# Second block: where the decay's exponentials stand on ScalarE, the pace of the chain of heads, and where the condition's rows live

## The chip, the cores and the metric

The kernel runs on one NeuronCore of one Trainium2 chip. The metric is the device time of one launch in microseconds (us), lower is better; the time before is the median of three runs. Engines are named as the profile names them: PE is TensorE (PEld its weight loads), DVE is VectorE, ACT is ScalarE, POOL is GpSimd, SP is SyncE, which here issues DMAs.

## The reference, cut to what matters

One sequence of 256 positions and 1024 channels goes through a first block of two layers and then a second block of two layers. The change is in the second block, but for one buffer of the first (`mod` below: the condition's rows). All matrix products are float32.

```
def first_block(x, c, ...):
    c_act = silu(c)
    for l in range(2):
        mod = c_act @ w_ada[l] + b_ada[l]      # the condition
        ...

def second_block(x, ...):
    for l in range(2):
        z = rms_norm(x) @ w_in[l]
        (cq, ckv, kpe, gq, gk, gv, glr, gr, su, gates) = split(z)
        o_a = mla_mixer(cq, ckv, kpe)          # 8 heads, causal softmax
        o_b = gla_mixer(gq, gk, gv, glr, gr)   # below
        o_c = s5_mixer(su)                     # diagonal state space, gelu, then a gated product w_glu
        g = sigmoid(gates + gate_b)            # 3 x 1024 wide
        x = x + (g0 * (o_a @ w_br_mla) + g1 * (o_b @ w_br_gla) + g2 * (o_c @ w_br_s5)) @ w_out[l]
        x = x + square(relu(rms_norm(x) @ w_ff1[l])) @ w_ff2[l]

def gla_mixer(q, k, v, g_lr, r):
    log_a = log_sigmoid(g_lr @ w_gate + b_gate) / 16
    bc = cumsum(log_a, within chunks of 64)
    q_t, k_t, k_end = q * exp(bc), k * exp(-bc), k * exp(bc_last - bc)
    ... # chunked products with v, a state carried over four chunks
```

## The kernel before

**Weights and products.** Weights stream from HBM in tiles of 128x1024 (`raw`, 5 buffers, loaded by SP). Each is split into two parts whose sum is the float32 value: `whi` by a copy on ACT (L463, 4 buffers) and `wlo = raw - whi` on DVE (L464, 3 buffers). `lin_t` computes one output tile of 128x256 from eight weight slices with 24 matmuls, three for each slice (L499, L500, L501); a product over four slices has 12. The results stand in one of four PSUM buffers (`pmm`); short products and transposes use four others (`px`). A fifth user of `pmm` has to wait until the first has been read.

**The second block's order.** `block2(l)` is written as a program, and a scheduler sets each engine's queue from it by readiness and priority; each engine then works its own queue in order. The projection `w_in_2` gives in turn the latents, the s5 input `u` and `gr`, then the sources of the attention's q, k and v (L1579 to L1585). Then, at L1596 to L1604, the decay: `log1pexp_neg` on DVE (L676 to L683), L1599, L1600 and eight cumulative sums (L1604, `TENSOR_TENSOR_SCAN`) into `bc`, followed by ten exponentials on ACT: `eb` (L1606), `en` (L1609) and eight pieces of `ke` (L1611). Their two 128x512 tiles are named `ge` in the profile. Then the values `gv` (`lin_n`, two `pmm` buffers) with two copies on ACT (L1617).

After that a loop over 24 gates: each is one `lin_t` (24 matmuls) and one tanh on ACT (L1693) that frees its `pmm`. Ahead of gate 4 stands `linear_qk` (four tiles, scaled by `eb`, `en` and `ke` on DVE). Ahead of each gate `paced(chain, CHAIN)` writes the next steps of a generator, `chains()`: eight steps of `mla_heads` (for each half of the heads, for q and k, for two row tiles: L1650, the rotary lines L805 to L811 and L1655 on DVE give `mq3`, which four transposes L689 turn two steps later and a copy L690 on ACT reads), then `gla` (L1772 to L1837: products `am`, the states `gst` as a chain of ACT and DVE steps, then the output), then the attention (L827 to L862). `paced` ties a step to the last matmul and the last `wlo` written so far.

At every third gate one step of `s5_run` is written. It has four rounds q = 0 to 3. A round is: four products L1464 with the tile `ur`; copies and products on ACT and DVE (L1466 to L1470); eight scans (L1475); copies and products again (L1477 to L1481) that end in `vb`; four matmuls L1489 and eight L1493; a copy `yj` (L1496); a DMA to HBM (L1497) and two back (L1500, issued by SP); and the update of `uT[:, q]` (L1504). What is left of the rounds after the gates is written after the branch products of gla and mla (eight tiles of 12 matmuls each). Then come gelu (L1717) and the split `yhlh` (L554) of each `uT[:, q]`, and the gated product `s5_w_glu_2` that contracts over the four q, q = 3 last (four tiles of 12 matmuls).

**Buffers.** `slot()` gives 128x1024 float32 tiles from a pool of `NSLOT` = 20. `crow`, the condition's rows of the first block, has a 128x1024 tile of its own for the whole program.

Of the kernel before, what the change touches and what calls it, by code (L numbers as in the profile page):

```python
# [19 lines left out]
F32 = mybir.dt.float32  # L20
F32R = mybir.dt.float32r
I32 = mybir.dt.int32
AF = mybir.ActivationFunctionType
# [325 lines left out]
def program(ctx: ExitStack, tc: tile.TileContext, a, out, pp_at, cst_at):  # L349
    nc = tc.nc  # L350
    V, S, G, PE, SY = nc.vector, nc.scalar, nc.gpsimd, nc.tensor, nc.sync

    cpool = ctx.enter_context(tc.tile_pool(name="cpool", bufs=1))
# [4 lines left out]
    ps_x = ctx.enter_context(tc.tile_pool(name="psx", bufs=1, space=bass.MemoryType.PSUM))  # L358
    dram = ctx.enter_context(tc.tile_pool(name="dram", bufs=1, space=bass.MemoryType.DRAM))

    NSLOT = 20
    NFILL = 4
    PUP = 6
    PDN = 2
# [4 lines left out]
    NTH = 2  # L369
    NSC = 2  # L370
    LAG = 2
    CHAIN = 2
    REST_AT = 6
    PRIO = 1500

# [13 lines left out]
    cact = cpool.tile([128, 8], F32, name="cact")  # L389
    xns = [slots.tile([128, 4, 256], F32, name="xn", tag="s4", bufs=NSLOT) for _ in range(2)]  # L390
    xns = [x.rearrange("p a b -> p (a b)") for x in xns]
# [16 lines left out]
    def P(key, j=None):  # L408
        o, n = pp_at[key]
        p, o = (pp[0], o) if o < PP0 else (pp[1], o - PP0)  # L410
        return p[:, o:o + n] if j is None else p[:, o + j:o + j + 1]
# [4 lines left out]
    def slot(dt=F32, name="s4"):  # L416
        return slots.tile([128, 4, 256], dt, name=name, tag="s4", bufs=NSLOT)

# [3 lines left out]
    def t256(name="t256", dt=F32):  # L422
        return tmp.tile([128, 256], dt, name=name, tag="t256", bufs=N256)
# [66 lines left out]
    def lin_t(name, src, kts, m=128, parts=(128,), n=T, ps=None):  # L490

        ps = pmm() if ps is None else ps
        kts = list(kts)
        for q, kt in enumerate(kts):
            if parts == (128,):
                wh, wl = weight(m, name)
            else:
                wh, wl = joined([(weight(c, name), st["last"])[1] for c in parts])
            PE.matmul(ps[:m, :n], wh, src.hi(kt), start=q == 0, stop=False)  # L499
            PE.matmul(ps[:m, :n], wh, src.lo(kt), start=False, stop=False)  # L500
            st["mm"] = PE.matmul(ps[:m, :n], wl, src.hi(kt), start=False, stop=q == len(kts) - 1).ins  # L501
        return ps

    def paced(gen, n=1):

        for _ in range(n):
            with tc.issue_after(st["mm"]), tc.issue_after(st["lo"]):
                next(gen, None)
# [17 lines left out]
    def lin_n(name, src, kts, n):  # L526

        ps = [pmm(), pmm()]
        kts = list(kts)
        for q, kt in enumerate(kts):  # L530
            add_n(ps, src, kt, weight(n, name), q == 0, q == len(kts) - 1)
        return ps
# [221 lines left out]
        V.tensor_reduce(norms[0].ss, sqs, AX.X, OP.add)  # L754


    crow = cpool.tile([128, 1024], F32, name="crow")
    for q in range(2):
        pc = px()
        for j in range(4):  # L760
# [745 lines left out]
    def block2(l):  # L1506
        w = "w_in_2"
        flat = lambda x: x.rearrange("p a b -> p (a b)")
# [86 lines left out]
        for j in range(2):  # L1595
            S.activation(la[:, j * 256:(j + 1) * 256], pa[:, j * 256:(j + 1) * 256], AF.Identity,  # L1596
                         bias=P(("bg", l), j))
# [4 lines left out]
        bc, eb = ges[:, 0:512], ges[:, 512:1024]  # L1602
        for q in range(8):
            V.tensor_tensor_scan(bc[:, q * 64:(q + 1) * 64], ones[:, :64], la[:, q * 64:(q + 1) * 64], 0.0,  # L1604
                                 OP.mult, OP.add)
        S.activation(eb, bc, AF.Exp)  # L1606
        ges2 = flat(slot(name="ge2"))
        en, ke = ges2[:, 0:512], ges2[:, 512:1024]
        S.activation(en, bc, AF.Exp, scale=-1.0)  # L1609
        for q in range(8):  # L1610
            S.activation(ke[:, q * 64:(q + 1) * 64], bc[:, q * 64:(q + 1) * 64], AF.Exp,  # L1611
                         bias=bc[:, q * 64 + 63:q * 64 + 64], scale=-1.0)
        next(steps)
        gv = flat(slot(name="gv"))
        gvN = [gv[:, t * 512:(t + 1) * 512] for t in range(2)]
        for t, p_ in enumerate(lin_n(w, h, range(8), 512)):
            S.activation(gvN[t], p_, AF.Copy)  # L1617
        gqk = slot(name="gqk")
        gqf, gkf = flat(gqk[:, 0:2, :]), flat(gqk[:, 2:4, :])

        def linear_qk():
            for j in range(2):
                js = slice(j * 256, (j + 1) * 256)
                ps = lin_t(w, h, range(8))
                V.scalar_tensor_tensor(gqf[:, js], ps[:, :T], 0.125, eb[:, js], OP.mult, OP.mult)
            for j in range(2):
                js = slice(j * 256, (j + 1) * 256)
                ps = lin_t(w, h, range(8))
                V.tensor_tensor(gkf[:, js], ps[:, :T], en[:, js], OP.mult)
                V.tensor_tensor(ke[:, js], ps[:, :T], ke[:, js], OP.mult)  # L1630
# [33 lines left out]
        def chains():  # L1664
            for hf in range(2):
                yield from mla_heads(hf)
            while late:
                yield
                f_, *args = late.pop(0)
                f_(*args)  # L1670
            ob.append(new_hl(4, "ob"))
            yield from gla(l, eb, gqf, gkf, ke, gvN, gr, ob[0])
            oa.append(new_hl(4, "oa"))
            yield from attention((0, 4), lambda hh: heads[hh // 4]["q"][:96, hh % 4, :],
                                 lambda hh: heads[hh // 4]["k"][:96, hh % 4, :], 96 ** -0.5,
                                 lambda t: C("caus")[:, 128 - 128 * t:],
                                 lambda t, hh: vs[:, hh // 4, t, hh % 4], oa[0])
# [4 lines left out]
        gates, chain = {}, chains()  # L1682
        for n in range(24):
            if n == GQK_AT:
                linear_qk()
            paced(chain, CHAIN)
            if n % 3 == 2:
                paced(steps)
            br, j = (1, 0, 2)[n // 8], n % 8
            if j % 4 == 0:  # L1690
                gates.setdefault(br, []).append(slot(name="gate"))
            ps = lin_t(w, h, range(8))
            S.activation(gates[br][j // 4][:, j % 4, :], ps[:, :T], AF.Tanh,  # L1693
                         bias=gbh[:, br * 8 + j:br * 8 + j + 1], scale=0.5)
# [27 lines left out]
        for j in range(4):  # L1722
            ps = lin_t("s5_w_glu_2", yhl, range(4))
            t = t256("oc")
# [117 lines left out]
    for l in range(2):  # L1842
        block2(l)
# [28 lines left out]
```

## Time and profile before

| | |
|---|---|
| median of three runs | 2246.64 us (2245.1 to 2252.94) |
| the profiled execution | 2245.79 us, span 2243.8 us |
| mean granted clock of PE | 0.98 of full speed |
| PE busy | 2140.3 us, 95% of the span |
| PEld busy | 2024.6 us, 90% |
| DVE busy | 1732.6 us, 77% |
| ACT busy | 1336.3 us, 60% |
| POOL busy | 116.5 us, 5% |

PE sets the time: what counts is where PE stands idle or runs at half clock, and that is read from the timeline of PE, from what ended its waits, and from short windows with their granted clock. The second block's layer 0 has its decay and gates at 1380 to 1530 us of the span, layer 1 at 1840 to 2010 us. A timeline row gives start, length, engine, line, operation, tiles, count, and in brackets the idle time just before and what ended it.

### The profile page before, as it was taken

The page shows a single profiled execution, that of the slowest core. Times are in us where ns is not written, and L with a number is a line of the kernel's source. Part 1 is how long each engine was busy: PE and PEld are TensorE (multiplying, and loading weights), DVE is VectorE, ACT ScalarE, POOL GpSimd, SP SyncE. Part 2 cuts the span into 40 slices and gives each one's busy share as a digit, 9 for nine tenths or more (in the row PEclk, how much of TensorE's full clock was granted, in tenths as well). Part 3 has the DMA queues.
Part 4 walks back from the last instruction along what each step waited for, and adds up shares of the span by engine and source line. Part 5 has one row for each costly group of instructions (what it writes and reads, how often), then busy time and mean ns, then how long its engine had stood idle before and what let it go on. Part 6 is the DMA issues. An engine that isn't in the chain of part 4 may idle for free. (4 is left out here: it accounts for less than half of the span.)

```text
span 2243.8 us, 44306 instructions
## 1 busy us (share of the span) xinstructions
PE 2140.3 (95%) x17296; PEld 2024.6 (90%) x17296; DVE 1732.6 (77%) x3349; ACT 1336.3 (60%) x2461; POOL 116.5 (5%) x122
## 2 busy tenths in 40 slices
PE   7998999999998997999989999899999997999999
PEld 6888789998997886889989998899999997999999
DVE  4888888889887888788889787677875577678753
ACT  4546866466646557775576566585664464755643
POOL 0210011000000210011000001000000010000000
PEclk9999999999999998999999999899999998999999
DMA  8755344856685653444746666444555564444553
GB/s 324 246 206 197 138 166 152 296 198 208 224 286 188 225 190 132 167 162 164 263 159 199 200 242 225 135 157 158 177 190 182 174 218 135 150 160 162 195 180 123
DMA packets 143457, 429.09 MB, mean 191 GB/s; under 512 B 34864, under 2 KB 40976, under 8 KB 143248
## 3 DMA queue, kind: packets, MB, share of 16 engines
q1 hardware_dynamic: 136496, 422.24, 55.4%
q10 hardware_dynamic: 6752, 4.02, 0.6%
q8 instruction: 136, 2.23, 0.4%
q14 instruction: 73, 0.60, 0.1%
HBM read 413.98 MB, written 12.22 MB: 190 GB/s over the span
## 5 line engine op out<-in xcount | busy, mean ns | idle before, releaser
L463 ACT ACTIVATE whi<-raw 128x1024 fp32r<-128x1024 f32 x639 | 674.8, 1059 | 592.4 <-PE pmm L500 356.1
L464 DVE TENSOR_TENSOR wlo<-raw,whi 128x1024 fp32r<-128x1024 f32 x639 | 781.8, 1225 | 295.0 <-PE pmm L501 161.8
L499 PE MATMUL pmm<-hh,whi 128*128 128x256 f32 x2432 | 698.3, 288 | 31.8 <-ACT fh L554 14.9
L501 PE MATMUL pmm<-hh,wlo 128*128 128x256 f32 x2432 | 693.0, 286 | 4.1 <-DVE wlo L464 4.1
L500 PE MATMUL pmm<-hl,whi 128*128 128x256 f32 x2432 | 694.2, 286 | 0.0
L499 PEld LDWEIGHTS pmm<-hh,whi 128*128 128x128 f32 x2432 | 470.0, 194 | 40.8 <-ACT fh L554 15.2
L501 PEld LDWEIGHTS pmm<-hh,wlo 128*128 128x128 f32 x2432 | 469.3, 194 | 9.2 <-DVE wlo L464 4.9
L500 PEld LDWEIGHTS pmm<-hl,whi 128*128 128x128 f32 x2432 | 470.5, 194 | 4.4 <-issue 3.8
L499 PE MATMUL pmm<-fh,whi 128*128 128x256 f32 x864 | 244.6, 284 | 2.1 <-ACT whi L463 2.0
L500 PE MATMUL pmm<-fl,whi 128*128 128x256 f32 x864 | 244.2, 283 | 0.0
L501 PE MATMUL pmm<-fh,wlo 128*128 128x256 f32 x864 | 243.5, 283 | 0.0
L499 PEld LDWEIGHTS pmm<-fh,whi 128*128 128x128 f32 x864 | 165.7, 192 | 2.8 <-ACT whi L463 2.5
L500 PEld LDWEIGHTS pmm<-fl,whi 128*128 128x128 f32 x864 | 165.7, 192 | 0.1
L501 PEld LDWEIGHTS pmm<-fh,wlo 128*128 128x128 f32 x864 | 165.3, 192 | 0.2
L560 POOL TENSOR_TENSOR rr<-rv,mhalf 128x2 f32<-128x2 f32 (+3 forms) x26 | 55.5, 2136 | 1173.3 <-DVE rv L565 1173.3
L523 PE MATMUL pmm<-wlo,hh 128*128 128x512 f32 x256 | 102.6, 403 | 0.0
L522 PE MATMUL pmm<-whi,hh 128*128 128x512 f32 x256 | 95.9, 403 | 1.7 <-ACT hh L548 1.5
L524 PE MATMUL pmm<-whi,hl 128*128 128x512 f32 x256 | 97.3, 398 | 0.0
L718 DVE SCALAR_TENSOR_TENSOR raw<-raw,crow 128x1024 f32<-128x1024 f32 x44 | 53.8, 1223 | 25.6 <-DMA raw<-in_ada 25.6
L499 PE MATMUL pmm<-yh,whi 128*128 128x256 f32 x256 | 71.6, 283 | 0.1
L500 PE MATMUL pmm<-yl,whi 128*128 128x256 f32 x256 | 71.5, 283 | 0.0
L501 PE MATMUL pmm<-yh,wlo 128*128 128x256 f32 x256 | 71.5, 284 | 0.0
(560 smaller groups left out, 4242.0 us busy)
## 6 DMA issues: line engine op xcount, KB each, us to landing
raw<-in_w SPq DMA_DIRECT2D x639, 512.0 KB, 4.1
raw<-in_ada SPq DMA_DIRECT2D x96, 512.0 KB, 4.5
csb<-csd SPq DMA_DIRECT2D x16, 512.0 KB, 5.7
phd<-phases SPq DMA_DIRECT2D x8, 512.0 KB, 2.9
phasel<-phd SPq DMA_DIRECT2D x8, 512.0 KB, 3.9
dpd<-dp SPq DMA_DIRECT2D x4, 512.0 KB, 3.7
gl<-gd SPq DMA_DIRECT2D x32, 64.0 KB, 3.4
bl<-in_s5b SPq DMA_DIRECT2D x4, 512.0 KB, 5.6
```

Of the source, the lines that this page charges most:

```text
L463: S.activation(hi, raw, AF.Copy)
L464: st["lo"] = V.tensor_tensor(lo, raw, hi, OP.subtract).ins
L499: PE.matmul(ps[:m, :n], wh, src.hi(kt), start=q == 0, stop=False)
L500: PE.matmul(ps[:m, :n], wh, src.lo(kt), start=False, stop=False)
L501: st["mm"] = PE.matmul(ps[:m, :n], wl, src.hi(kt), start=False, stop=q == len(kts) - 1).ins
L522: PE.matmul(ps[t][:, :n], src.hi(kt)[:, ts], w[0], start=start, stop=False)
L523: PE.matmul(ps[t][:, :n], src.hi(kt)[:, ts], w[1], start=False, stop=False)
L524: st["mm"] = PE.matmul(ps[t][:, :n], src.lo(kt)[:, ts], w[0], start=False, stop=stop).ins
L560: G.tensor_tensor(r, v, mhalf.to_broadcast([128, n]), OP.pow)
L718: V.scalar_tensor_tensor(w, w, 1.0, crow, OP.mult, OP.mult, accum_out=m)
```

## The change

Three things. `CHAIN`, a number, becomes a row of numbers by gate: no step of the chain ahead of gate 0, one ahead of each of gates 1 to 5, two from gate 6 on. The ten exponentials are written after the `gv` copies, in `issue_after(gv_out)`, so behind the second copy on ACT; the tile `ge2` that they write is taken from the slots after `gv`. And `crow` becomes a slot, with `NSLOT` raised from 20 to 21. Lines after L1605 get other numbers: the copies of `gv` are L1610, the exponentials L1615, L1616 and L1618, the tanh of a gate is L1695.

```
--- before.py
+++ after.py
@@ -358,7 +358,7 @@
     ps_x = ctx.enter_context(tc.tile_pool(name="psx", bufs=1, space=bass.MemoryType.PSUM))
     dram = ctx.enter_context(tc.tile_pool(name="dram", bufs=1, space=bass.MemoryType.DRAM))
 
-    NSLOT = 20
+    NSLOT = 21
     NFILL = 4
     PUP = 6
     PDN = 2
@@ -369,7 +369,7 @@
     NTH = 2
     NSC = 2
     LAG = 2
-    CHAIN = 2
+    CHAIN = (0,) + 5 * (1,) + 18 * (2,)
     REST_AT = 6
     PRIO = 1500
 
@@ -754,7 +754,7 @@
         V.tensor_reduce(norms[0].ss, sqs, AX.X, OP.add)
 
 
-    crow = cpool.tile([128, 1024], F32, name="crow")
+    crow = slot(name="crow").rearrange("p a b -> p (a b)")
     for q in range(2):
         pc = px()
         for j in range(4):
@@ -1603,18 +1603,20 @@
         for q in range(8):
             V.tensor_tensor_scan(bc[:, q * 64:(q + 1) * 64], ones[:, :64], la[:, q * 64:(q + 1) * 64], 0.0,
                                  OP.mult, OP.add)
-        S.activation(eb, bc, AF.Exp)
-        ges2 = flat(slot(name="ge2"))
-        en, ke = ges2[:, 0:512], ges2[:, 512:1024]
-        S.activation(en, bc, AF.Exp, scale=-1.0)
-        for q in range(8):
-            S.activation(ke[:, q * 64:(q + 1) * 64], bc[:, q * 64:(q + 1) * 64], AF.Exp,
-                         bias=bc[:, q * 64 + 63:q * 64 + 64], scale=-1.0)
         next(steps)
         gv = flat(slot(name="gv"))
         gvN = [gv[:, t * 512:(t + 1) * 512] for t in range(2)]
         for t, p_ in enumerate(lin_n(w, h, range(8), 512)):
-            S.activation(gvN[t], p_, AF.Copy)
+            gv_out = S.activation(gvN[t], p_, AF.Copy).ins
+        ges2 = flat(slot(name="ge2"))
+        en, ke = ges2[:, 0:512], ges2[:, 512:1024]
+
+        with tc.issue_after(gv_out):
+            S.activation(eb, bc, AF.Exp)
+            S.activation(en, bc, AF.Exp, scale=-1.0)
+            for q in range(8):
+                S.activation(ke[:, q * 64:(q + 1) * 64], bc[:, q * 64:(q + 1) * 64], AF.Exp,
+                             bias=bc[:, q * 64 + 63:q * 64 + 64], scale=-1.0)
         gqk = slot(name="gqk")
         gqf, gkf = flat(gqk[:, 0:2, :]), flat(gqk[:, 2:4, :])
 
@@ -1683,7 +1685,7 @@
         for n in range(24):
             if n == GQK_AT:
                 linear_qk()
-            paced(chain, CHAIN)
+            paced(chain, CHAIN[n])
             if n % 3 == 2:
                 paced(steps)
             br, j = (1, 0, 2)[n // 8], n % 8
```

The order of instructions in the first block is the same on every engine; the second block's differs in both layers. ACT in layer 0, from the last weights ahead of the values to the first gates, before (the second 128x512 tile of `ge` has a number behind it):

```order
L463 ACTIVATE whi<-raw 128x1024 x4
L1611 ACTIVATE ge_17152<-ge 128x64 x7
L1606 ACTIVATE ge<-ge 128x512
L1609 ACTIVATE ge_17152<-ge 128x512
L1611 ACTIVATE ge_17152<-ge 128x64
L1617 ACTIVATE gv<-pmm 128x512 x2
L1693 ACTIVATE gate<-pmm,gbh 128x256
L690 ACTIVATE mqT<-px 96x4x128
L1693 ACTIVATE gate<-pmm,gbh 128x256
```

and after:

```order
L463 ACTIVATE whi<-raw 128x1024 x4
L1610 ACTIVATE gv<-pmm 128x512 x2
L1618 ACTIVATE ge_17268<-ge 128x64 x7
L1615 ACTIVATE ge<-ge 128x512
L1616 ACTIVATE ge_17268<-ge 128x512
L1618 ACTIVATE ge_17268<-ge 128x64
L1695 ACTIVATE gate<-pmm,gbh 128x256 x2
L463 ACTIVATE whi<-raw 128x1024
L1695 ACTIVATE gate<-pmm,gbh 128x256
```

The two `gv` copies moved ahead of the ten exponentials; the first gates' tanhs stay behind the exponentials, and the copies of the heads' transposes (L690) are no longer between them.

DVE in layer 0, the end of the decay's chain with the heads' steps between, before:

```order
L807 TENSOR_TENSOR mq_17353<-ru,rv 128x4x16
L811 TENSOR_TENSOR mq_17353<-ru,rv 128x4x16
L682 SCALAR_TENSOR_TENSOR lp<-lp,z_17128 128x512
L1650 TENSOR_TENSOR mq_17372<-mk,rows 128x4x64
L807 TENSOR_TENSOR mq_17372<-ru,rv 128x4x16
L811 TENSOR_TENSOR mq_17372<-ru,rv 128x4x16
L1655 TENSOR_TENSOR mq_17353<-mq_17353,rr 128x384
L683 SCALAR_TENSOR_TENSOR lp<-lp,z 128x512
L1655 TENSOR_TENSOR mq_17372<-mq_17372,rr 128x384
L1599 SCALAR_TENSOR_TENSOR la<-la,lp 128x512
L1600 TENSOR_SCALAR la<-la 128x512
L1604 SCALAR_TENSOR_TENSOR ge<-ones,la 128x64 x8
```

and after:

```order
L682 SCALAR_TENSOR_TENSOR lp<-lp,z_17128 128x512
L807 TENSOR_TENSOR mq_17326<-ru,rv 128x4x16
L811 TENSOR_TENSOR mq_17326<-ru,rv 128x4x16
L682 SCALAR_TENSOR_TENSOR lp<-lp,z_17128 128x512
L1657 TENSOR_TENSOR mq_17326<-mq_17326,rr 128x384
L682 SCALAR_TENSOR_TENSOR lp<-lp,z_17128 128x512
L683 SCALAR_TENSOR_TENSOR lp<-lp,z 128x512
L1599 SCALAR_TENSOR_TENSOR la<-la,lp 128x512
L1600 TENSOR_SCALAR la<-la 128x512
L1604 SCALAR_TENSOR_TENSOR ge<-ones,la 128x64 x8
L464 TENSOR_TENSOR wlo<-raw,whi 128x1024
L1652 TENSOR_TENSOR mq_17371<-mq,rows 128x4x64
```

Ahead of the eight scans stood four of the heads' steps that end in L1655 (two of them seen here), and now one (L1657); in layer 1 there were six, and now two.

PE in layer 0, around the last round (q = 3) of s5, where `oah` and `obh` are the attention's and gla's outputs in the branch products and `yhlh` is the gated product's source; before:

```order
L501 MATMUL pmm<-obh,wlo 128x256
L1493 MATMUL px<-vb,dpl 64x64 x8
L499 MATMUL pmm<-obh,whi 128x256
L500 MATMUL pmm<-obl,whi 128x256
L501 MATMUL pmm<-obh,wlo 128x256
```

and after:

```order
L501 MATMUL pmm<-yhlh,wlo 128x256
L1493 MATMUL px<-vb,dpl 64x64 x8
L499 MATMUL pmm<-yhlh,whi 128x256 x4
L500 MATMUL pmm<-yhll,whi 128x256
L501 MATMUL pmm<-yhlh,wlo 128x256
```

The eight L1493 of q = 3 stood inside the gla branch, with 111 matmuls of the branches and the gated product between them and the first matmul that needs q = 3 of `yhlh`; now they stand directly ahead of the four that need it. The four L1464 of q = 3 moved from among the last gates' matmuls to the first tiles of the mla branch. Layer 1 has 75 matmuls between before, and none after.

## Rows read from the trace of the kernel before

**Rows 1.** Waits of PE, whole span: us, times, longest.

```profile
PE pmm L499 <- ACT gv L1617: 12.3, 2, 7.4
```

**Rows 2.** Timeline of PE, layer 0, then layer 1.

```profile
1398.85 0.28 PE L500 MATMUL pmm<-hl,whi 128*128 128x256 f32 x1
1398.97 0.28 PE L501 MATMUL pmm<-hh,wlo 128*128 128x256 f32 x1
1403.76 2.10 PE L689 MATMUL px<-cst,mq 128*96 128x128 f32 x8 [4.51 <-DVE mq L1655]
1407.66 1.09 PE L689 MATMUL px<-cst,mq 128*96 128x128 f32 x4 [1.79 <-DVE mq L1655]
1413.69 0.58 PE L499 MATMUL pmm<-hh,whi 128*128 128x256 f32 x1 [4.94 <-ACT gv L1617]
...
1857.69 2.10 PE L689 MATMUL px<-cst,mq 128*96 128x128 f32 x8 [4.78 <-DVE mq L1655]
1862.13 1.09 PE L689 MATMUL px<-cst,mq 128*96 128x128 f32 x4 [2.34 <-DVE mq L1655]
1870.60 0.58 PE L499 MATMUL pmm<-hh,whi 128*128 128x256 f32 x1 [7.38 <-ACT gv L1617]
```

**Rows 3.** Windows of PE: length, busy (count), granted clock, DMA share, GB/s.

```profile
1416.00:1418.00 2.00, 2.00 (x12) 0.60 0.00 0
...
1874.00:1876.00 2.00, 2.00 (x15) 0.76 0.00 0
```

**Rows 4.** Timeline of ACT, layer 0, then layer 1.

```profile
1397.78 1.06 ACT L463 ACTIVATE whi<-raw 128x1024 fp32r<-128x1024 f32 x1 [1.87 <-DVE wlo L464]
1410.10 1.78 ACT L1611 ACTIVATE ge<-ge 128x64 f32<-128x64 f32 x7 [11.26 <-DVE ge L1604]
...
1413.06 1.06 ACT L1617 ACTIVATE gv<-pmm 128x512 f32<-128x512 f32 x2
1414.02 0.46 ACT L1693 ACTIVATE gate<-pmm,gbh 128x256 f32<-128x256 f32 x1
...
1852.83 1.06 ACT L463 ACTIVATE whi<-raw 128x1024 fp32r<-128x1024 f32 x1 [1.82 <-PE pmm L500]
1867.01 1.78 ACT L1611 ACTIVATE ge<-ge 128x64 f32<-128x64 f32 x7 [13.12 <-DVE ge L1604]
```

**Rows 5.** Timeline of DVE in layer 0: one step of a head, then the scans.

```profile
1406.45 0.42 DVE L1650 TENSOR_TENSOR mq<-mk,rows 128x256 f32<-128x256 f32 x1
1406.78 0.22 DVE L807 TENSOR_TENSOR mq<-ru,rv 128x64 f32<-128x64 f32 x1
...
1407.06 0.55 DVE L1655 TENSOR_TENSOR mq<-mq,rr 128x384 f32<-128x384 f32 x1
1407.52 0.68 DVE L683 SCALAR_TENSOR_TENSOR lp<-lp,z 128x512 f32<-128x512 f32 x1
...
1409.77 1.56 DVE L1604 TENSOR_TENSOR_SCAN ge<-ones,la 128x64 f32<-128x64 f32 x8
```

**Rows 6.** Windows: length, busy of PE, PEld, DVE, ACT, POOL, clock, DMA share, GB/s.

```profile
1440.00:1530.00 90.00, 90.00 (x797) 85.15 (x796) 59.39 (x117) 68.20 (x143) 2.59 (x7) 1.00 0.44 150
1900.00:2010.00 110.00, 110.00 (x970) 104.71 (x970) 76.52 (x149) 75.90 (x150) 2.36 (x4) 1.00 0.45 149
```

**Rows 7.** Page part 5, the group of `wlo`; then timeline of DVE, s5 round q = 2.

```profile
L464 DVE TENSOR_TENSOR wlo<-raw,whi 128x1024 fp32r<-128x1024 f32 x639 | 781.8, 1225 | 295.0 <-PE pmm L501 161.8
...
1501.31 0.68 DVE L1468 TENSOR_TENSOR zr<-px,phasel 128x512 f32<-128x512 f32 x1
```

**Rows 8.** Timeline of ACT, then DVE: last round trip of s5 in layer 1.

```profile
2000.72 0.37 ACT L1496 ACTIVATE yj<-px 128x256 f32<-128x256 f32 x1
2008.01 0.42 ACT L554 ACTIVATE yhlh<-uT 128x256 fp32r<-128x256 f32 x1
...
2006.83 0.69 DVE L1504 SCALAR_TENSOR_TENSOR uT<-uT,pp,yt 128x256 f32<-128x256 f32 x1 [0.99 <-DMA yt<-yd]
```

**Rows 9.** Timeline of PE after the gated product, layer 1.

```profile
2015.30 1.22 PE L499 MATMUL pmm<-och,whi 128*128 128x256 f32 x4 [3.14 <-ACT och L551]
```

More of the change, by code (lines that the diff above doesn't have):

```diff
@@ L359, in program @@
     dram = ctx.enter_context(tc.tile_pool(name="dram", bufs=1, space=bass.MemoryType.DRAM))
-    NSLOT = 20
+    NSLOT = 21
     NFILL = 4
@@ L371, in program @@
     LAG = 2
-    CHAIN = 2
+    CHAIN = (0,) + 5 * (1,) + 18 * (2,)
     REST_AT = 6
@@ L754, in program @@
         V.tensor_reduce(norms[0].ss, sqs, AX.X, OP.add)
-    crow = cpool.tile([128, 1024], F32, name="crow")
+    crow = slot(name="crow").rearrange("p a b -> p (a b)")
     for q in range(2):
@@ L1605, in block2 @@
                                  OP.mult, OP.add)
[L1606 to L1612, printed above, removed]
         next(steps)
@@ L1616, in block2 @@
         for t, p_ in enumerate(lin_n(w, h, range(8), 512)):
-            S.activation(gvN[t], p_, AF.Copy)
+            gv_out = S.activation(gvN[t], p_, AF.Copy).ins
+        ges2 = flat(slot(name="ge2"))
+        en, ke = ges2[:, 0:512], ges2[:, 512:1024]
+        with tc.issue_after(gv_out):
+            S.activation(eb, bc, AF.Exp)
+            S.activation(en, bc, AF.Exp, scale=-1.0)
+            for q in range(8):
+                S.activation(ke[:, q * 64:(q + 1) * 64], bc[:, q * 64:(q + 1) * 64], AF.Exp,
+                             bias=bc[:, q * 64 + 63:q * 64 + 64], scale=-1.0)
         gqk = slot(name="gqk")
@@ L1685, in block2 @@
                 linear_qk()
-            paced(chain, CHAIN)
+            paced(chain, CHAIN[n])
             if n % 3 == 2:
```

## The prediction

> **What bounds the kernel now.** PE is busy for 95% of the span, so a change off PE pays only where PE waits. I read the waits of PE first, then its timeline in the second block, then short windows for the clock, and last what ACT and DVE did while PE waited. PE waits twice for the copies of `gv`, 12.3 us in all [rows 1]. The timeline shows these two waits in a cluster with four others of the heads' transposes: idle 4.51, 1.79 and 4.94 us in layer 0 and 4.78, 2.34 and 7.38 us in layer 1 [rows 2], so 11.2 and 14.5 us. The clock falls as well. The window 1416 to 1418 has a granted clock of 0.60 and 1874 to 1876 one of 0.76 [rows 3]; with the two levels 1.2 and 2.4 GHz that is half speed until about 1417.6 and 1875.0. PE had resumed at 1413.69 and 1870.60 [rows 2], so it worked 3.9 and 4.4 us at half speed and lost half of that, 1.95 and 2.2 us. The twelve transposes took 2.10 and 1.09 us at half speed, of which 1.6 us in each layer is the clock's. The lost time is 14.8 us in layer 0 and 18.3 us in layer 1, **33.1 us together**. This is the ceiling of any gain.
>
> Why PE waits: ACT stands for 11.26 and 13.12 us in front of the first exponential, waiting for the scans [rows 4], with the `gv` copies and the first tanhs queued behind it, while all four `pmm` buffers are full. The scans are late because four steps of the heads (six in layer 1) lie ahead of them on DVE. Everywhere else PE is full: 90.00 us of 90 and 110.00 of 110 in the rest of the gates and branches, at clock 1.00 [rows 6]. These two stretches have no room to gain and much to lose.
>
> The Trainium skill, page "TensorE: Matmul & The Clock Gate", section "Terms", prices a slow clock as the slow time times one minus the clock's ratio. With slow stretches of about 13.6 and 17 us that is 15.3 us where the rows give 7.4; by it the loss before would be 41 us and the forecast below 8 us lower. The rows decide here, since PE stood idle for most of that time.
>
> **The change part by part.** *The copies of `gv`.* They now wait only for the last `whi`, which ends at 1398.84 and 1853.89 [rows 4]; the first copy is done 0.55 us later. PE ended gate 1 at 1399.25 and 1852.91 (start minus idle) [rows 2], so it waits 0.2 and 1.6 us. Then gates 2 and 3 run, 48 matmuls at 0.12 us (the step of two neighbours) [rows 2], 5.8 us, until 1405.2 and 1860.3.
>
> *The wait that takes their place.* The next tile, the first of `linear_qk`, needs the buffer of gate 0, whose tanh stands behind the exponentials. A head's step costs DVE 0.33 for L1650, six short ones of 0.14 and 0.46 for L1655, so 1.63 us [rows 5]. Three fewer of them bring the scans of layer 0 from 1409.77 to 1404.9; four fewer bring those of layer 1 from 1866.7 (0.33 ahead of the exponentials' 1867.01, as in layer 0 [rows 4, 5]) to 1860.2, and I add 0.5 us for steps that now follow each other back to back. From the scans' start to the end of the exponentials are 3.29 us, and the tanh takes 0.46 [rows 4, 5]. Gate 0 is read at 1408.7 and 1864.5, and PE waits 3.5 and 4.2 us. Idle here: 3.7 and 5.8 us, 9.5 in all. For the clock I take 1.9 us for each layer, the price read above; the bounds are 0 and 2.2. A wait of 3.14 us was followed by four matmuls in 1.22 us [rows 9], far from 0.12 each, so a wait of this length does slow the clock. **Sum 13.3 us.**
>
> *The chain of heads, later by a gate.* What was six steps in the gap is now beside gates and `linear_qk`, on a DVE with 59 to 77 us of work in 90 to 110 [rows 6]; the transposes follow two steps later, and the matmuls of the gates in between cover them. I cost them at nothing; without the cover each would show like the 1.79 to 4.78 us of today. But gla starts later too, and its states now run beside round q = 1 of s5. Between the first `gst` and the last one DVE gets six products and sums of the round at 0.6, its scans (1.56) and a `wlo` (1.2) [rows 5, 7], 6.4 us, and PE has hardly 2 us of its own between the states' products in layer 1. Row and order allow 0 (before, nothing waits there [rows 6]) to 4.5 us in each layer; I take 3. **Sum 6 us.**
>
> *The last round of s5.* This is the part that the words of the change don't say. The L1464 of q = 3 come later by about 150 matmuls, and nothing stands on PE between its L1493 and the matmuls that need `yhlh` of q = 3. What used to run under 111 and 75 matmuls (13.3 and 9.0 us) is now in the open. From the start of `yj` to the end of `yhlh` are 2008.43 - 2000.72 = 7.7 us: copy, DMA out, DMA back, L1504 at 2006.83, gelu, split [rows 8]; with 0.3 us of handing over, 8 us of idle in each layer, **16 us**. Bounds are 7 and 9.5, an estimate: the 0.99 us that L1504 waits for the landing may shrink, and a `whi` of 1.06 [rows 4] may stand in ACT's way. Ahead of it L1493 waits for `vb`. The chain from L1464 to `vb` is two copies and six products at 0.6 us [rows 7] and eight scans, 1.56 like those of rows 5, so 6.4 us; on DVE stand between them three `wlo` at 1.2 [rows 7] and some fifteen steps of the branches at 0.33, the price of L1650 with as many elements [rows 5]. That is 15 us of work, and I add 1.5 for the steps that wait for PE. PE has 108 matmuls there, 13 us, and the four short ones of L1489. That gives 3 us in each layer, bounds 0 and 4: **6 us**. After 8 us of idle the clock falls: 1.95 in each layer, **4 us**, bounds 0 and 4.4. Last, in layer 0 the order behind the gated product becomes that of layer 1, in which PE waited 3.14 us for `och` [rows 9]; before, other matmuls stood between. **3 us**, bounds 0 and 3; layer 1 has it already.
>
> The Trainium skill, page "DMA: Bandwidth & Descriptors", section on the anatomy of a DMA, gives about 2.0 us as the fixed cost of one. Two of them would be 4 us, against the 6.1 us from `yj` to L1504 in the rows; the round trip would be up to 2 us shorter in each layer and the forecast 4 us lower. The trace has its own duration, so it is used.
>
> *`crow` in a slot.* The first block keeps its 20 other slots and its order on every engine; it reads and writes the same bytes. Nothing, between -1 and 1 us.
>
> **The sum.** After: 13.3 + 6 + 16 + 6 + 4 + 3 = 48.3 us lost, before 33.1, so 15.2 us more. Made against the profiled execution (2245.79 us, 0.85 under the median of 2246.64, so the two can stand for one another): 2261.0 us, slower by 0.7%. With every bound at its low end the loss is 23.5 us and the time 2236; at its high end some 58 us and 2271.
>
> **The rivals.**
>
> *Even.* Only what the order forces happens: the waits for gate 0 (13.3) and the round trips with their clock (20), 33.3 us, against 33.1 before. The states of gla and `vb` come in time, since before they did [rows 6]. Time 2246, and 2240 to 2257 with the clock's bounds and a part of the other waits. Against it: the sums of DVE's work are longer than PE's cover in both places. Chance 0.34.
>
> *Faster.* The round trip of q = 3 stays hidden. The place is PE between the L1493 of q = 3 and the first matmul on its `yhlh`; it decides from 8 / 0.12 = 66 ready matmuls on. Then the loss is 13.3 us and up to 6 at gla, and the time 2245.8 - 33.1 + 13.3 to 19.3 = 2226 to 2232. For it: the waits that the words of the change aim at are there and go in large part. Against it: PE takes its queue in order, as its idle 4.94 us in front of one L499 show [rows 2], and the order has no matmul there. Chance 0.08.
>
> *Slower still.* The four tanhs of the gates ahead of the attention stand on ACT behind the last reader of an old `ur` tile, whose slot the gates take, and hold all four `pmm`; any delay of round q = 1 then stops PE directly. Priced by the longest such wait of today, 4.9 us for each layer: 2271. It lies on the forecast's side; of its chance 0.58 about 0.1 is this.
>
> **How the numbers follow.** Forecast 2261, chance 0.58 with the last rival; even 0.34; faster 0.08. The measurement tells about 0.5%, 11 us, from no change: faster is below 2235.4, slower above 2257.9. Faster 0.08, same 0.34, slower 0.58. The range leaves out 0.2: it runs from 2243, inside the even case, to 2272.
>
> **What would show it.** Right: the waits of PE on `gv` fall from 12.3 to under 2.5 us, a wait for a gate's tanh (L1695) of 3 to 5 us appears in each layer at about 1405 and 1860, ACT's first exponentials start near 1405 and 1861, and PE stands idle for about 8 us in each layer ahead of L499 on `yhlh`, some 160 us after the gates begin, with a clock of 0.50 behind it. Small waits for `gst` and `vb` add up to about 12 us. Wrong: no wait of 7 us or more before `yhlh` (then faster), scans that start no earlier than before, or new waits of some us inside the attention, which I cost at nothing.

## The result, and the profile after

The changed kernel takes 2259.14 us (median of 6 runs, 2255.68 to 2265.93), the kernel before 2246.31 us (6 runs, 2241.66 to 2252.94). The ratio is 1.0056, 95% interval 1.0036 to 1.0076: slower by some 13 us, forecast 2261.0. PE's share stays at 95%:

```profile
span 2253.7 us, 44283 instructions
PE 2148.1 (95%) x17296; PEld 2031.7 (90%) x17296; DVE 1733.2 (77%) x3349; ACT 1337.3 (59%) x2461; POOL 114.8 (5%) x122
```

The length of the first block differs from execution to execution: in the fourteen traces of this case its end, read as the start of the first L1539, lies between 1346 and 1363 us. So traces are compared by the second block alone, from that instruction to the end of the span. It takes 891.1 us before (1352.7 to 2243.8) and 907.6 us after (1346.1 to 2253.7).

The view of PE's waits, over the whole span (us, times, longest), shows what came in place of [rows 1] and of the waits for `mq` in [rows 2], which are gone:

```profile
PE pmm L499 <- ACT yhlh L554: 13.6, 2, 6.8
PE pmm L499 <- ACT gate L1695: 7.5, 2, 4.0
PE pmm L499 <- ACT och L551: 4.9, 2, 2.6
PE pmm L499 <- DVE gate L1704: 2.6, 4, 1.2
PE px L1493 <- DVE vb L1481: 1.7, 2, 1.4
PE pmm L499 <- ACT gv L1610: 1.5, 1, 1.5
PE px L1815 <- DVE gst L1799: 1.0, 1, 1.0
```

The timeline of PE puts them in their places, layer 0 first (start, length, engine, line, operation, tiles, count, idle before and what ended it):

```profile
1402.47 0.58 PE L499 MATMUL pmm<-hh,whi 128*128 128x256 f32 x1 [3.57 <-ACT gate L1695]
1453.53 0.43 PE L1815 MATMUL px<-gqk,gst 128*128 128x64 f32 x2 [0.47 <-ACT gst L1796]
1454.49 0.66 PE L1489 MATMUL px<-ur,toep 128*64 128x128 f32 x8 [0.25 <-ACT osq L1820]
1552.27 1.22 PE L499 MATMUL pmm<-yhlh,whi 128*128 128x256 f32 x4 [6.84 <-ACT yhlh L554]
1557.55 1.22 PE L499 MATMUL pmm<-och,whi 128*128 128x256 f32 x4 [2.36 <-ACT och L551]
...
1866.51 0.58 PE L499 MATMUL pmm<-hh,whi 128*128 128x256 f32 x1 [3.95 <-ACT gate L1695]
2011.52 0.69 PE L1493 MATMUL px<-vb,dpl 128*64 128x64 f32 x16 [1.44 <-DVE vb L1481]
2018.94 1.22 PE L499 MATMUL pmm<-yhlh,whi 128*128 128x256 f32 x4 [6.73 <-ACT yhlh L554]
```

So the cluster of six waits at the start of the two layers (25.7 us of idle, [rows 2]) has shrunk to 3.57 us in layer 0 and 1.5 and 3.95 in layer 1. The last round of s5, which cost PE nothing before, is now open twice, for 6.84 and 6.73 us.

The timeline of ACT shows both: at the start the exponentials wait 5.69 us for the scans, where they waited 11.26 [rows 4], and the two tanhs that PE needs come behind them; at the end PE waits through the whole chain from `yj` to `yhlh`:

```profile
1399.00 1.78 ACT L1618 ACTIVATE ge<-ge 128x64 f32<-128x64 f32 x7 [5.69 <-DVE ge L1604]
1401.96 0.81 ACT L1695 ACTIVATE gate<-pmm,gbh 128x256 f32<-128x256 f32 x2
...
1545.47 0.39 ACT L1496 ACTIVATE yj<-px 128x256 f32<-128x256 f32 x1 [6.05 <-PE px L1493]
1551.80 0.42 ACT L554 ACTIVATE yhlh<-uT 128x256 fp32r<-128x256 f32 x1
```

From the start of `yj` to the end of `yhlh` are 6.75 us. Last, windows of PE with the granted clock (after the busy times of PE, PEld, DVE, ACT and POOL stand the clock, the DMA share and GB/s). The first is the start of layer 0, the next two are gla in layers 0 and 1, the last is the end of layer 0:

```profile
1401.00:1408.00 7.00, 5.53 (x26) 5.31 (x27) 5.03 (x15) 5.38 (x11) 0.00 (x0) 0.52 0.51 164
1455.00:1459.00 4.00, 4.00 (x34) 3.67 (x31) 1.43 (x4) 2.23 (x6) 0.00 (x0) 0.57 0.73 201
1920.00:1927.00 7.00, 7.00 (x47) 6.76 (x46) 0.71 (x3) 1.99 (x6) 0.00 (x0) 0.54 0.57 164
1548.00:1561.00 13.00, 6.38 (x28) 6.08 (x29) 6.14 (x12) 5.51 (x12) 0.00 (x0) 0.50 0.29 91
```

The start ran at the lower clock before as well [rows 3]. New is the lower level, 1.2 GHz, in three places that ran at full speed before: gla of both layers, inside the stretches of [rows 6], and the end of layer 0; at the end of layer 1 it lasts longer. What the clock costs is counted here in windows of 1 us, as half of PE's busy time at the lower level. In the second block that makes 8.5 us before and 16.9 us after. PE's idle time in the second block grew only from 37.5 to 41.4 us (its length less PE's busy time). Idle and clock together are 12.3 us of the 16.5 by which the second block is longer; the other 4 us are not located.

### The profile page after: what moved, and what is told of

Read it like the earlier page. It is cut to its first block, busy times and chain, and to the rows that moved or that the text cites. A ratio compares the mean times of both kernels' runs of the same rounds, so it can differ in the third digit from the quotient of the medians.

```text
span 2253.7 us, 44283 instructions
## 1 busy us (share of the span) xinstructions
PE 2148.1 (95%) x17296; PEld 2031.7 (90%) x17296; DVE 1733.2 (77%) x3349; ACT 1337.3 (59%) x2461; POOL 114.8 (5%) x122
## 5 line engine op out<-in xcount | busy, mean ns | idle before, releaser
L499 PE MATMUL pmm<-hh,whi 128*128 128x256 f32 x2432 | 697.8, 288 | 28.3 <-ACT fh L554 14.8
L499 PEld LDWEIGHTS pmm<-hh,whi 128*128 128x128 f32 x2432 | 469.9, 194 | 36.6 <-ACT fh L554 15.2
L499 PE MATMUL pmm<-fh,whi 128*128 128x256 f32 x864 | 244.6, 284 | 2.1 <-ACT whi L463 2.1
L499 PEld LDWEIGHTS pmm<-fh,whi 128*128 128x128 f32 x864 | 165.7, 192 | 2.9 <-ACT whi L463 2.6
L499 PE MATMUL pmm<-yh,whi 128*128 128x256 f32 x256 | 71.6, 283 | 0.0
```

## Experiments: which part does what

Theory: the two edits pull against each other. The exponentials behind the copies are a gain, the late chain of heads is a loss, since it delays the heads, gla and, behind them, the last round of s5; the slot for `crow` does nothing. Rival: the exponentials only exchange one wait for another, and the loss at the end comes from the order that they bring.

**The exponentials alone.** The chain's pace stays at 2 from gate 0, and `crow` keeps its own tile.

```diff
-        S.activation(eb, bc, AF.Exp)
         ...
         for t, p_ in enumerate(lin_n(w, h, range(8), 512)):
-            S.activation(gvN[t], p_, AF.Copy)
+            gv_out = S.activation(gvN[t], p_, AF.Copy).ins
+        with tc.issue_after(gv_out):
+            S.activation(eb, bc, AF.Exp)
             ...
```

> Only the exponentials move behind the copies of gv; two steps of the chain ahead of every gate, 20 slots, crow in its own tile, as before. Theory (the move gains by itself, the pace loses): the waits on gv (4.9 and 7.4 us) vanish, the waits for the heads' transposes (6.3 and 7.1 us) stay, nothing moves at the end of s5: 12 us less, 2234 us (2229 to 2239). Rival (the move only swaps the wait on gv for one on a gate's tanh, and it needs the later chain to pay): 2246 us, within 3.

Measured: 2233.56 us (2231.29 to 2237.19), ratio 0.9943 (0.9923 to 0.9962), against 2246.37 for before on the same chip. PE's waits:

```profile
PE px L689 <- DVE mq L1657: 13.7, 5, 4.8
PE pmm L499 <- ACT och L551: 3.1, 1, 3.1
```

The waits for `gv` are gone, those for `mq` are as in [rows 2], and there is none for a gate's tanh, for `gst` or for `yhlh`. The exponentials still come late, behind the scans, and gate 0's tanh behind them; the rows of ACT, then of PE, in layer 0:

```profile
1410.69 1.79 ACT L1618 ACTIVATE ge<-ge 128x64 f32<-128x64 f32 x7 [10.29 <-DVE ge L1604]
...
1413.66 0.46 ACT L1695 ACTIVATE gate<-pmm,gbh 128x256 f32<-128x256 f32 x1
...
1408.99 0.56 PE L499 MATMUL pmm<-hh,whi 128*128 128x256 f32 x1
...
1415.71 0.28 PE L499 MATMUL pmm<-hh,whi 128*128 128x256 f32 x1
```

But PE, held up by the transposes, begins gates 2 and 3 only at 1408.99 us and comes to the buffer of gate 0 at 1415.71, after that tanh. The second block takes 879.0 us, 12.1 less than before; 12.3 is what [rows 1] had for `gv`.

**The pace alone** (with the slot), the exponentials left ahead of the copies.

```diff
-    NSLOT = 20
+    NSLOT = 21
-    CHAIN = 2
+    CHAIN = (0,) + 5 * (1,) + 18 * (2,)
-    crow = cpool.tile([128, 1024], F32, name="crow")
+    crow = slot(name="crow").rearrange("p a b -> p (a b)")
-            paced(chain, CHAIN)
+            paced(chain, CHAIN[n])
```

> Only the chain's pace and the 21 slots with crow among them; the exponentials stay ahead of the copies of gv. Theory (the pace costs what the late s5 round and gla cost): at the start the scans come about 5 us sooner, so PE idles some 21 us in both layers in place of 25.7 and the clock costs 4 in place of 7.4, 8 us gained; the waits at gla, ahead of yhlh and och come as in the changed kernel, about 30 us lost: 2268 us (2260 to 2275). Rival (the losses come from the exponentials' new place): 2238 us.

Measured: 2266.41 us (2264.27 to 2268.95), ratio 1.0088 (1.0068 to 1.0108). PE's waits:

```profile
PE pmm L499 <- ACT gv L1617: 21.4, 2, 11.6
PE pmm L499 <- ACT yhlh L554: 13.8, 2, 7.1
```

The waits for the transposes are gone, but PE spends what they gave in one long wait for `gv` in each layer, and the wait for `yhlh` is there without the exponentials having moved. So the rival falls: the loss at the end belongs to the pace. With the late pace, moving the exponentials gains 2266.4 - 2259.1 = 7.3 us, without it 12.8: with the late pace PE comes to gate 0's buffer at 1398.90 us (1402.47 - 3.57) and has to wait for that tanh.

**The slot alone.**

```diff
-    NSLOT = 20
+    NSLOT = 21
-    crow = cpool.tile([128, 1024], F32, name="crow")
+    crow = slot(name="crow").rearrange("p a b -> p (a b)")
```

> Only crow in a slot and 21 slots. Theory: nothing, 2246 us within 3, and the first block as long as before (the second block's first L1539 near 1352 us of the span). Rival (in the profile of the changed kernel that line came at 1346.1, 6.6 us sooner, and the slot did it): 2240 us.

Measured: 2247.08 us (2239.76 to 2252.62), ratio 0.9998 (0.9982 to 1.0014); the second block takes 892.1 us against 891.1. The slot costs and gives nothing.

## Experiments: taking the new waits away

**s5 earlier.** If the late last round is what costs, writing its steps at earlier gates must bring back nearly all of it: as the program reads, the products of q = 3 stand behind the last short products of the attention in the ring of four `px` buffers, which are taken in the order of the program. No run changes the ring itself.

```diff
             paced(chain, CHAIN[n])
-            if n % 3 == 2:
+            if n in (2, 5, 8, 11, 13, 15, 17, 19):
                 paced(steps)
```

> The changed kernel with the last three steps of s5 written ahead of gates 15, 17 and 19 in place of 17, 20 and 23, so that the px buffers of round q = 3 are taken ahead of the attention's last ones; all else as in the change. Theory (the loss is the open round trip of q = 3): the waits of 6.8 and 6.7 us on yhlh, the ones on vb and och beside them and the slow clock behind go, about 22 us: 2237 us (2231 to 2244). Rival (the late attention costs the time, wherever s5 stands): waits of the same size inside the attention or at its end, 2252 to 2260 us.

(Four steps move: beside the three that are named there, the one at gate 14 goes to 13.) Measured: 2243.28 us (2234.88 to 2251.85), ratio to before 0.9983 (0.9966 to 0.9999); second block 886.9 us, 20.7 less than the changed kernel. No wait for `yhlh` is left; the L1493 of q = 3 stand some 150 instructions earlier in PE's queue. Of the waits that the change brought, the largest that are left (all of PE's waits for a tanh, two of them the start's 3.57 and 4.0):

```profile
PE pmm L499 <- ACT gate L1695: 11.0, 4, 4.0
```

So the open round, with its clock and the `och` behind it, is worth 15.9 us by the medians and some 18 to 21 by the second blocks of the traces, in any case more than the whole loss of the change. A third wait, of 2.83 us at 1510 us of layer 0, ahead of a product of the gla branch, is new and takes some of it back; the fourth is 0.66 us. ACT was busy for 8.26 of the 8.65 us ahead of the tanhs that PE waits for at 1510 us, with steps of the attention, two table loads of 1.28 us and the copies of an s5 round: they stood in its queue behind these.

**The exponentials behind the tanh of gate 1.** In the changed kernel the tanhs of the first two gates wait behind them. Here they are written after gate 1.

```diff
-        with tc.issue_after(gv_out):
+        def decay_exps(behind):
+            with tc.issue_after(behind):
         ...
-            S.activation(gates[br][j // 4][:, j % 4, :], ps[:, :T], AF.Tanh,
+            th = S.activation(gates[br][j // 4][:, j % 4, :], ps[:, :T], AF.Tanh,
         ...
+            if n == 1:
+                decay_exps(th)
```

> The changed kernel with the exponentials behind the tanh of gate 1 in place of the second copy of gv. Theory (the first tile of linear_qk waits for gate 0's tanh only because it is queued behind the exponentials): the waits on a gate's tanh of 3.6 and 4.0 us go, with the slow clock behind them (2.8 and 2.7 us), the rest stays: 13 us under the changed kernel, 2246 us (2241 to 2251). Rival (the tile would wait for its own weights, whose wlo stands behind the scans on DVE): 3 us or less gained, 2256 us.

Measured: 2258.05 us (2252.63 to 2261.93), ratio 1.004 (1.0019 to 1.0062), second block 905.2 us. The waits for a tanh are gone and nearly nothing is gained. The row of PE in layer 0 says why, and under it the issues of SP (a queue's own time) in this kernel:

```profile
1413.50 1.08 PE L1464 MATMUL px<-ur,wst 128*128 128x128 f32 x4 [5.09 <-DMA ur<-ud]
...
1401.33 5.92 SPq L1426 DMA_DIRECT2D toep<-kd  x8
1407.29 1.25 SPq L1454 DMA_DIRECT2D ur<-ud  x2
1409.35 0.34 SPq L460 DMA_DIRECT2D raw<-in_w  x1
1409.73 3.75 SPq L1454 DMA_DIRECT2D ur<-ud  x6
```

The products of the first s5 round, written at gate 2, need `ur`, whose loads SP issues behind the eight for `toep`. In the changed kernel the same six issues end at 1405.5 us and L1464 starts at 1405.57, behind the wait for the tanh: the one wait had hidden the other. Counted from the first L1539, this L1464 starts at 59.4 us in both kernels. In layer 1 it is 59.7 and 58.4 us, so 1.3 us are gained there. My theory expected the gain and was wrong; the rival had the time but another reason.

**Both.**

> Both repairs: exponentials behind the tanh of gate 1, and the last three steps of s5 written ahead of gates 15, 17 and 19. Theory (the two losses are separate): the sum of the two gains, 13 and 21 us in the second block, 2228 us (2222 to 2234). Rival (what is saved at the start is waited for again later, since DVE is the slower one there): 2238 us or more.

Measured: 2242.92 us (2236.59 to 2252.62), ratio 0.9976 (0.9959 to 0.9993), second block 887.2 us: no better than s5 earlier by itself, and not the 2228 us of my theory. The waits for `ur` stay (5.3 and 3.4 us), since the steps of s5 that the start meets did not move.

## Experiments: a version that is faster than both

The next kernels keep the exponentials behind gate 1 and give the chain a short start only, `CHAIN = (0, 1, 1) + 21 * (2,)`, so that attention and gla end earlier. They differ in the gates at which a step of s5 is written: every third gate (v3), or

```diff
-            if n % 3 == 2:
+            if n in (5, 7, 9, 11, 14, 17, 20, 23):     # v5
+            if n in (5, 8, 10, 12, 14, 17, 20, 23):    # v6
```

> Exponentials behind the tanh of gate 1, and the chain with no step ahead of gate 0, one ahead of gates 1 and 2, two from gate 3 on, so that it is three steps less late than in the change; s5 paced as before the change. Theory: the start has no waits but 1.5 us on gv, 33 us of the loss before go, the round q = 3 has 73 and 78 matmuls ahead of its first reader, and gla costs 2 to 8 us: 2219 us (2213 to 2227). Rival (the heads' steps fill DVE and the tiles of linear_qk wait for wlo or for the transposes): 2230 us.

Measured: 2241.48 us (2235.42 to 2244.89), ratio 0.9968 (0.9954 to 0.9982), second block 890.9 us. That is 14 us above the end of my range. The waits for `yhlh` are gone but for 0.2 us, those for `ur` are still there (8.4 us in all). And the clock fell at gla in both layers, for ten microseconds of full work each:

```profile
1460.00:1471.00 11.00, 11.00 (x65) 10.53 (x64) 2.07 (x3) 2.79 (x4) 1.64 (x1) 0.53 0.45 140
1914.00:1925.00 11.00, 11.00 (x67) 10.53 (x67) 1.65 (x5) 3.36 (x9) 0.00 (x0) 0.53 0.47 151
```

> As the run before (exponentials behind the tanh of gate 1, chain with one step ahead of gates 1 and 2 and two from gate 3), but the eight steps of s5 at gates 5, 7, 9, 11, 14, 17, 20 and 23 in place of every third, so that the first L1464 stands some 180 matmuls later. Theory (L1464 of q = 0 stopped PE for 5.3 and 3.1 us on the DMA of ur because everything ahead of it had become quick): these waits and the slow clock behind the first go, 11 us under the run before, 2230 us (2224 to 2237). Rival (what is saved there comes back at gla, where PE, DVE and ACT pass small steps on to each other and the clock fell): 2241 us.

> As v5, with the steps of s5 at gates 5, 8, 10, 12, 14, 17, 20 and 23: rounds q = 0 and q = 1 stand elsewhere against the states of gla. Theory: the wait on ur is gone here as well, 2230 us (2224 to 2237); the half clock at gla, some 10 us long in the run before, is shorter where no L1493 stands between the states' products. Rival: the half clock at gla comes as before and the time is that of the run before, 2241 us.

Measured: v5 2221.71 us (2217.45 to 2225.35), ratio 0.9886 (0.9868 to 0.9904), second block 869.1 us; v6 2220.51 us (2216.61 to 2222.7), ratio 0.9879 (0.9859 to 0.9898), second block 866.0 us. Both are faster than either kernel of this case, by some 25 us against before and 38 us against the change, and faster than I expected of them: with the first s5 step at gate 5 the loads of `ur` have landed, and in the one trace of each the half clock at gla did not come back either. Of the waits that this text speaks of v6 has two left, and its windows (start and rest of layer 0, then of layer 1) are at nearly full speed:

```profile
PE pmm L499 <- ACT och L551: 5.1, 2, 3.1
PE pmm L499 <- ACT gv L1610: 1.5, 1, 1.5
...
1350.00:1450.00 100.00, 99.21 (x769) 93.65 (x768) 81.51 (x172) 63.05 (x114) 13.09 (x20) 1.00 0.66 210
1450.00:1560.00 110.00, 107.47 (x886) 101.48 (x886) 81.19 (x161) 75.76 (x148) 2.07 (x4) 0.98 0.47 151
1800.00:1900.00 100.00, 97.77 (x770) 93.34 (x769) 80.92 (x172) 63.64 (x113) 8.97 (x9) 1.00 0.63 203
1900.00:2020.00 120.00, 115.81 (x954) 109.87 (x953) 90.50 (x180) 78.90 (x157) 1.51 (x3) 0.99 0.47 152
```

## Experiments: does the order decide the clock?

At gla the clock fell in the changed kernel behind 0.47 and 0.25 us of idle, and in the kernel with s5 earlier it did not, behind the same instructions of PE and the same idle:

```profile
1453.74 0.43 PE L1815 MATMUL px<-gqk,gst 128*128 128x64 f32 x2 [0.47 <-ACT gst L1796]
1454.71 0.66 PE L1489 MATMUL px<-ur,toep 128*64 128x128 f32 x8 [0.25 <-ACT osq L1820]
...
1450.00:1460.00 10.00, 9.28 (x88) 8.33 (x87) 7.13 (x19) 6.37 (x14) 0.00 (x0) 1.00 0.53 155
```

So three kernels were profiled a second time, unaltered.

> The changed kernel once more, unaltered, for the clock alone. Its first trace has half speed at gla in both layers, 1455.7 to 1458.9 and 1919.8 to 1926.5 us, 1.7 and 3.4 us lost, though PE stood idle there for 0.7 and 1.5 us only. Theory A, the order of the work decides: half speed at the same places, lost time 1.7 and 3.4 us within 0.5, idle as before. Theory B, an execution decides (where else the clock was low, how the DMAs fell): the idle times stay at 0.7 and 1.5 us, but the time at half speed is another, 0 in at least one layer or over 1 us more or less.

> The kernel with the s5 steps at the gates 2, 5, 8, 11, 13, 15, 17, 19 once more, unaltered, for the clock alone. Its first trace has in layer 0 at gla the same instructions and the same idle (0.47 and 0.25 us) as the changed kernel, with the clock at 1.00, and in layer 1 half speed with 3.3 us lost. Theory A, the order decides: 0 and 3.3 us again. Theory B, an execution decides: half speed in layer 0 now, or none in layer 1.

> The kernel with the exponentials behind the tanh of gate 1 and no slow start of the chain, s5 at every third gate, once more, unaltered, for the clock alone. Its first trace has half speed for 10 us at gla in each layer, 5.1 us lost in each, with 1.3 us of idle. Theory A: 5.1 and 5.1 again, and a time near its median of 2241.5. Theory B: other numbers; if both layers stay at full speed, the time is about 10 us under that median.

Measured, the second trace of the changed kernel (2258.83 us): its rows of PE at the start, then windows at the start of layer 0, at gla of layer 0 and at gla of layer 1.

```profile
1408.38 0.39 PE L499 MATMUL pmm<-hh,whi 128*128 128x256 f32 x1 [3.57 <-ACT gate L1695]
...
1411.54 0.68 PE L1464 MATMUL px<-ur,wst 128*128 128x128 f32 x4 [1.35 <-DMA ur<-ud]
...
1405.00:1413.00 8.00, 3.27 (x26) 3.10 (x27) 6.88 (x22) 7.31 (x18) 0.00 (x0) 1.00 0.57 126
1459.00:1465.00 6.00, 5.74 (x62) 5.18 (x61) 3.60 (x7) 3.71 (x8) 0.00 (x0) 1.00 0.65 180
...
1922.00:1929.00 7.00, 6.47 (x44) 5.84 (x44) 2.22 (x6) 2.77 (x8) 0.00 (x0) 0.51 0.72 228
```

The waits of the first trace are there again, the same to a hundredth: 3.57 us for the tanh, 0.72 us of idle at gla of layer 0 and about 1.49 in layer 1. One is added, 1.35 us for `ur` at the start. The clock isn't the same. Lost to it are, from the start of layer 0 to the end of layer 1, in six stretches:

| | start 0 | gla 0 | end 0 | start 1 | gla 1 | end 1 | sum |
|---|---|---|---|---|---|---|---|
| changed kernel, first trace | 2.6 | 1.7 | 3.3 | 2.7 | 3.4 | 3.2 | 16.9 |
| changed kernel, second trace | 0 | 0 | 4.5 | 1.6 | 3.2 | 3.2 | 12.5 |

At the start of layer 0 full speed won nothing: PE came to L1464 sooner and waited there for `ur`, and L1464 starts 59.4 and 59.5 us behind L1539 in the two traces. The second block is 2.8 us shorter in the second trace, not 4.4.

The kernel with s5 earlier kept its pattern at gla (0 in layer 0, in layer 1 4.9 us where it was 3.3), but not at the start of layer 0 (0, then 1.6 us) nor behind the wait at 1510 us (1.7, then 0). v3 lost 5.1 us in layer 0 again, and 3.4 in layer 1 where it was 5.1; its time was 2251.55 us, above its earlier ones, and 8.5 us of that lie in the first block (its end at 1356.5 us, where it was 1348.0). So theory A falls for the changed kernel and holds in part elsewhere. The order decides where PE's work has gaps, but whether the clock falls at a gap, and for how long, differs between executions of one program, at these places by 0 to 3 us. What decides it there is not shown.

## Why the prediction was right

**The time.** 2261.0 forecast, 2259.14 measured. The sum came out by its terms only in part: two groups of them were off by about the same amount, with opposite signs. So the direction and the waits behind it were forecast, but that the two times lie within 2 us of each other is luck. In us for both layers, measured in the first trace:

| term | forecast | measured |
|---|---|---|
| start, idle (`gv` and the first tanh) | 9.5 | 9.0 |
| start, clock | 3.8 | 5.3 |
| gla, waits | 6 | 2.2 |
| gla, clock | 0 | 5.1 |
| `vb` and the branches' waits ahead of L1493 | 6 | 4.3 |
| `yhlh` round trip | 16 | 13.6 |
| clock at the end | 4 | 6.5, of which layer 1 had 1.5 before |
| `och` in layer 0 | 3 | 2.4 |

**Right: the start.** The step that shifts the scans by the heads' steps and puts exponentials and tanh behind them gave 3.5 and 4.2 us of waiting; it was 3.57 and 3.95. (The 0.5 us for steps back to back went into layer 1 alone; with it layer 0 would have had 4.0.) `gv` 0.2 and 1.6; it was none and 1.5. The transposes, costed at nothing, cost nothing: no wait for `mq` is left. The wait for `ur`, which stands directly behind, was not in the forecast.

**Right: the round trip at the end,** which the words of the change don't name. The pace alone brings it and earlier s5 steps remove it, so it is shown. Its size was 1.2 us too large in each layer, so the waits of 6.84 and 6.73 us fall short of the "7 us or more" without which the prediction would have called itself wrong: that line was drawn too close to the forecast. I took 7.7 us from [rows 8], and after the change the same chain takes 6.75 in layer 0. The first DMA makes the difference: from its issue to the issue of the second were 2.7 us before (2001.12 to 2003.83), and 1.7 us in both layers after. The DMA engines' share was 0.83 then (2001 to 2004) and 0.23 after (1545.9 to 1547.6); that this is the reason is not shown.

The Trainium skill, page "DMA: Bandwidth & Descriptors", section on the anatomy of a DMA, gives about 2.0 us as a DMA's fixed cost, so two make 4.0, an estimate. The section is about DMAs that GpSimd issues, and the two here are issued by ACT and SP, so the prediction should not have priced them by it without saying so. From the start of `yj` to L1504 the changed kernel takes 1550.65 - 1545.47 = 5.2 us, of which 0.39 is `yj` itself. That is nearer to the estimate than the 6.1 of [rows 8], and still 0.8 us above it.

**Off: gla.** I took 3 us of waiting in each layer, in the middle of 0 to 4.5; it was 0.7 and 1.5. DVE's steps between the states had more cover on PE than I saw: in layer 1, from the first `gst` on DVE (1912.64 us) to the start of the last L1815 (1919.64), PE was idle for 1.48 of 7.0 us, so it had 5.5 us of work there where I counted 2.

**Off: the clock, the largest error.** I forecast 7.8 us and the trace has 16.9, or 12.5 in the second one. The step that failed is "1.95 in each layer" for each long wait and nothing for the short ones. Behind `yhlh` the clock does not come back before `och` is waited for, so in layer 0 one low stretch covers both waits, and in layer 1 a second follows the first; and at gla the clock fell behind waits of 0.25 to 0.95 us, which I had costed without one. By the table idle was forecast 9.0 us too high, and the clock 9.1 too low, or 7.6 without the 1.5 us that layer 1 lost there before. The two errors cancel, and that is why the sum stands: 48.3 us forecast, 46.9 measured by the terms, against 33.1 before.

The Trainium skill, page "TensorE: Matmul & The Clock Gate", section "Terms", prices a slow clock by the slow time, times one half. The stretch 1548 to 1561 has 13.0 us at 0.50, so 6.5 us by the page, an estimate; PE was busy for 6.38 of it, and half of that is 3.2. Where PE never stops, as in v3 from 1460 to 1471, page and rows agree: 11.0 times (1 - 0.53) is 5.2, again an estimate, and the windows of 1 us give 5.1. So the rule holds for full work, and the idle part has to be taken out, as the forecast did. Its "8 us lower" used the rule for before alone; used for both traces, with 34 us of low clock before and 48 after, the rule gives 17 and 24 us, an estimate, where PE's busy time gives 8.5 and 16.9.

**The rivals.** *Even* (2246) lacked the `vb` and `gla` terms and `och`; the rows show these at 2.2 + 4.3 + 2.4 = 8.9 us, and the clock. *Faster* (2226 to 2232) needed ready matmuls between L1493 of q = 3 and L499: there are none, but v5 and v6, which have them, run at 2221. *Slower still* (2271) did not come: no `pmm` was held by tanhs behind an old `ur` slot in the changed kernel. With s5 earlier PE did wait 2.83 us more for a tanh, at 1510 us, but ACT was busy nearly all the time ahead of it, so it stood behind other work and not behind a slot.

## What to carry to other kernels

When a late producer is given room by delaying another chain, follow that chain to its last consumer: here the heads' chain, as the program reads, held the ring of `px` buffers, and its delay surfaced 150 us later, where the last DMA round trip lost its cover. Try each half of such a change alone; one half was a gain of 13 us, the other a loss of 20. And a wait that goes may have hidden another that ends just before it: look up what else the same instructions need, and when that lands.

## What the runs showed of the hardware

That a program and its waits do not settle the granted clock: one kernel was at full speed behind 3.57 us of idle in one execution and at half speed for 5 us behind the same wait in the other, and at gla of layer 0, with waits equal to a hundredth of a microsecond, at full speed in one and at half speed for 3 us in the other (12.5 and 16.9 us lost in all). And half speed came at gla behind waits of 0.25 to 1.28 us in the middle of full work, in v3 for some 10 us in three of four places. I had thought of it as following waits of 3 us and more, as in [rows 9]. Nor does lost clock add up to lost time: at the start of layer 0 the next wait, for `ur`, took back what full speed had given.

The Trainium skill, page "TensorE: Matmul & The Clock Gate", section "What's actually happening", says that the number of slow matmuls at the start of one kernel varies from run to run. The two traces of the changed kernel show such a spread in the middle of a kernel, 12.5 and 16.9 us. A forecast of a few tenths of a per cent carries that spread, here about 4 us.
